# Operand sums of the value products built three half items sooner, with the fourth sum ahead of the first, and two dilated heads begun three half items later

## The chip, the cores and the metric

One core of a Trainium2 chip runs the whole kernel. The time is in device microseconds (us) of that core, from runs of the same program; a profiled execution gives the span and the trace. Engines are named as in the profile: PE (TensorE, matmuls), PEld (its weight loads), DVE (VectorE), ACT (ScalarE), POOL (GpSimd), SP (SyncE, which issues loads).

## The reference

One layer of a decoder trunk on 512 tokens and 1024 channels. Cut to what matters here:

```python
proj = x @ w_in                       # one projection; its columns are q/k/v of three mixers and three gates
(da_q, da_k, da_v, sb_q, sb_k, sb_v, dl_q, dl_k, dl_v, gates) = jnp.split(proj, ...)
o_da = diff_attention(da_q, da_k, da_v, lam, ...)          # 4 heads, two softmax maps each
o_sb = stick_breaking_attention(sb_q, sb_k, sb_v)          # 8 heads
o_dl = dilated_attention(dl_q, dl_k, dl_v, ...)            # 3 groups x 4 heads; groups (128,1),(512,4),(2048,16)
g = sigmoid(gates)
m = (g0 * (o_da @ w_branch_da) + g1 * (o_sb @ w_branch_sb) + g2 * (o_dl @ w_branch_dil)) @ w_out
x = layer_norm(alpha * x + m)
x = layer_norm(alpha * x + relu(x @ w_up)**2 @ w_down + sigmoid(x @ w_ple_gate) * (p @ w_ple))
```

A dilated head slot takes its logits in three groups, softmaxes each, and adds the three group outputs with weights that come from their softmax denominators. The output is float32.

## The kernel before

**Products.** Each float32 operand is split into a high part (ACT casts it to fp32r) and a low part (DVE subtracts), and each product of a 128-row block is three matmuls: high by high, high by low, low by high. Weights come through SP into a ring of 7 tiles `raw`; `split_next` writes the two parts `wh` (L214, ACT) and `wl` (L216, DVE) into rings of 6 tiles each, so a cast waits until PE has left the tile six before it.

**The items.** The work of PE is a list of items, mostly one 128-column or 128-token product of the projection each. The loop at the end of `trunk` goes through them; before each item, and once in the middle of a long one, it calls `step()`, which moves every active generator on to its next `yield`. A `yield` in a generator is therefore half an item of waiting. The attention heads (`sb_head`, `dil_head`, `da_block`) and the helpers in `pending` are such generators. The order that stands in the program on each engine is then made by a scheduler and is fixed; at run time each engine takes its instructions in that order and waits at the first that is not ready.

**The value products.** `value_pair` computes two of the three dilated value projections (`dl_v` 1 and 2) with seven products in place of eight, numbered p and taken in the order 2, 1, 7, 6, 4, 5, 3, each for two token halves r of 12 matmuls (L426 to L428). Products 2, 1 and 3 use x as it is; 7, 6, 4 and 5 need sums of blocks of x. `value_forms` makes these: x comes by POOL's queue into eight tiles `xr` (L353); sum 7 (L376, four DVE instructions), sum 6 (L369), sum 1 (L388, it goes into product 5) and sum 4 (L369 again) go into tiles `fr`, and `parts` casts each to `u7h`, `u6h`, `u4h`, `u5h` on ACT (L239) and takes the low parts `u7l` to `u5l` on DVE (L240). The results are added up by DVE (L436, L440, L441, L443, L447); products 2 and 7 are copied out of their PSUM bank by ACT (L433).

**A dilated head.** `dil_head(hd)` goes in these steps, a `yield` between them: the logits of group 0 on PE (L1589; L1592 in the changed file), whose masked maxima DVE takes (L1592; L1595) and whose exponentials ACT takes; the logits of groups 1 and 2 (L1605; L1608) with DVE's maxima (L1613; L1616); two small products with `fold` and `foldT` (L1630, L1632; L1633, L1635) that bring the statistics of the groups together; a chain of small DVE instructions and one exponential (L1636 to L1652; L1639 to L1655), then eight scalings of the logits (L1654, L1658; L1657, L1661); transposes on PE (L1673, L1682, the same lines in both files) with copies out by ACT and DVE (L98, L100); and the products with the values (L1694, L1699). Heads 0 and 1 run beside the value products.

**Tiles.** Most of these tiles come from one pool of 46 slots of 128x512 (`slot`). A new tile takes a slot that an older one has left, and its first writer waits for the older tile's last reader. PSUM has 2 banks `mm` and 6 banks `at`, with the same rule.

The lines that are not in the functions below:

```python
        RING, RAW = 6, 7
        NSLOT = 46
            if n == v_from[0]:
                pending.append(value_forms())      # four items ahead of value_pair's first
```

## Time and profile before

| | |
|---|---|
| three runs, median | 1066.5 us (1065.89 to 1066.74) |
| profiled execution, its own time | 1067.35 us |
| its span, first to last instruction | 1065.6 us |
| PE, PEld busy | 1049.0 us (98%), 905.1 us (85%) |
| DVE, ACT, POOL busy | 774.1 us (73%), 568.5 us (53%), 145.8 us (14%) |
| granted TensorE clock over the span | 0.995 |

The profiled execution took 0.85 us more than the median; 1.75 us of its time lie outside the span. Busy time is an average over stages. The change touches a stretch from about 225 to 300 us after the span's start, and there the trace has to be read instruction by instruction.

### The profile page before, as it was taken

What the parts mean: (1) busy time and instruction counts of PE and PEld (TensorE: products, weight loads), DVE (VectorE), ACT (ScalarE), POOL (GpSimd) and SP (SyncE); (2) the same over time, 40 slices, a digit from 0 to 9 for tenths busy, and PEclk for the clock granted to TensorE, in tenths of its full rate; (3) what the DMA queues carried; (4) which work ended last, traced back from release to release, by engine and by line L of the source; (5) the groups of instructions that cost most, each with busy time, mean ns of one, the idle gap of its engine ahead of it and who ended that gap; (6) DMA issues with size and microseconds to landing.
All of it is one profiled execution on the core that took longest, in us unless ns stands there. A gap on an engine that the chain in (4) does not pass through costs nothing.

```text
span 1065.6 us, 15588 instructions
## 1 busy us (share of the span) xinstructions
PE 1049.0 (98%) x5802; PEld 905.1 (85%) x5802; DVE 774.1 (73%) x1383; ACT 568.5 (53%) x991; POOL 145.8 (14%) x224
## 2 busy tenths in 40 slices
PE   9999999999899999999999999999999999999996
PEld 6887788889788888888999988888999889889885
DVE  6887667649844757769768773888677877877965
ACT  6665445526432546547535452675756665666641
POOL 0001401220212103230111130100101100100000
PEclk9999999999899999999999999999999999999999
DMA  8346767974898819982676693148888978776602
GB/s 315 111 150 228 168 198 190 306 265 126 234 325 248 241 40 286 243 240 81 204 192 197 180 308 125 62 138 296 225 300 261 242 246 264 244 237 235 196 22 79
DMA packets 63260, 219.75 MB, mean 206 GB/s; under 512 B 7912, under 2 KB 8824, under 8 KB 63184
## 3 DMA queue, kind: packets, MB, share of 16 engines
q1 hardware_dynamic: 37056, 126.80, 34.1%
q0 software_dynamic: 25552, 91.04, 32.9%
q8 instruction: 45, 0.74, 0.3%
q10 hardware_dynamic: 576, 0.92, 0.2%
q14 instruction: 31, 0.25, 0.1%
HBM read 216.61 MB, written 81.81 MB: 280 GB/s over the span
## 4 chain that ended last, share of the span: by engine, by line
PE 88%; DVE 7%; issue 2%; ACT 2%; DMA 0%; POOL 0%; SPq 0%; DVEq 0%; POOLq 0%; ACTq 0%
PE mm L89 13%; PE mm L91 13%; PE mm L90 13%; PE at L89 4%; PE at L1076 4%; PE at L1077 4%; PE at L1078 4%; PE at L91 4%; PE at L90 4%; DVE wl L216 2%; PE mm L458 2%; PE mm L460 2%; PE mm L459 2%; PE at L133 1%; PE at L1467 1%
## 5 line engine op out<-in xcount | busy, mean ns | idle before, releaser
L214 ACT CAST wh<-raw 128x1024 fp32r<-128x1024 f32 x249 | 256.7, 1035 | 262.8 <-PE mm L90 158.7
L216 DVE TENSOR_TENSOR wl<-raw,wh 128x1024 fp32r<-128x1024 f32 x249 | 298.5, 1205 | 99.1 <-ACT wh L214 96.4
L89 PE MATMUL mm<-xhT,wh 128*128 128x512 f32 x368 | 146.7, 399 | 0.0
L91 PE MATMUL mm<-xhT,wl 128*128 128x512 f32 x368 | 144.4, 393 | 0.0
L90 PE MATMUL mm<-xlT,wh 128*128 128x512 f32 x368 | 144.0, 391 | 0.0
L91 PEld LDWEIGHTS mm<-xhT,wl 128*128 128x128 f32 x368 | 69.1, 188 | 15.0 <-DVE wl L216 0.3
L89 PEld LDWEIGHTS mm<-xhT,wh 128*128 128x128 f32 x368 | 69.2, 188 | 13.7 <-issue 0.4
L90 PEld LDWEIGHTS mm<-xlT,wh 128*128 128x128 f32 x368 | 69.2, 188 | 12.9
L1076 PE MATMUL at<-wh,hh 128*128 128x512 f32 x188 | 73.7, 392 | 0.0
L1077 PE MATMUL at<-wl,hh 128*128 128x512 f32 x188 | 73.7, 392 | 0.0
L89 PE MATMUL mm<-x1hT,wh 128*128 128x256 f32 x256 | 73.7, 288 | 0.0
L1078 PE MATMUL at<-wh,hl 128*128 128x512 f32 x188 | 73.1, 389 | 0.0
L90 PE MATMUL mm<-x1lT,wh 128*128 128x256 f32 x256 | 72.3, 283 | 0.0
L91 PE MATMUL mm<-x1hT,wl 128*128 128x256 f32 x256 | 71.9, 283 | 0.0
L89 PEld LDWEIGHTS mm<-x1hT,wh 128*128 128x128 f32 x256 | 48.8, 191 | 4.7 <-ACT up L1010 2.7
L90 PEld LDWEIGHTS mm<-x1lT,wh 128*128 128x128 f32 x256 | 48.9, 191 | 1.5
L914 POOL DMA_DIRECT2D usum<-in_wu_dram x32 | 28.5, 891 | 152.3 <-DVE wl L216 126.6
L91 PEld LDWEIGHTS mm<-x1hT,wl 128*128 128x128 f32 x256 | 48.6, 191 | 0.0
L914 POOL DMA_DIRECT2D dsum<-in_wd_dram x28 | 24.9, 890 | 130.9 <-DVE wl L216 96.2
L1078 PEld LDWEIGHTS at<-wh,hl 128*128 128x128 f32 x188 | 35.3, 188 | 7.7
L1076 PEld LDWEIGHTS at<-wh,hh 128*128 128x128 f32 x188 | 35.5, 189 | 6.0
L1077 PEld LDWEIGHTS at<-wl,hh 128*128 128x128 f32 x188 | 35.5, 189 | 5.5
(516 smaller groups left out, 2666.7 us busy)
## 6 DMA issues: line engine op xcount, KB each, us to landing
usum<-in_wu_dram POOLq DMA_DIRECT2D x48, 512.0 KB, 7.9
raw<-in_wt_dram SPq DMA_DIRECT2D x46, 512.0 KB, 5.1
dsum<-in_wd_dram POOLq DMA_DIRECT2D x42, 512.0 KB, 8.3
raw<-usum SPq DMA_DIRECT2D x32, 512.0 KB, 4.7
raw<-dsum SPq DMA_DIRECT2D x28, 512.0 KB, 4.5
raw<-in_wd_dram SPq DMA_DIRECT2D x25, 512.0 KB, 4.3
raw<-in_wu_dram SPq DMA_DIRECT2D x24, 512.0 KB, 5.2
raw<-in_wv_dram SPq DMA_DIRECT2D x18, 512.0 KB, 8.5
```

The lines of the kernel that those rows point to most:

```text
L89: nc.tensor.matmul(ps, wh, xh, start=start, stop=False, skip_group_check=True)
L90: nc.tensor.matmul(ps, wh, xl, start=False, stop=False, skip_group_check=True)
L91: nc.tensor.matmul(ps, wl, xh, start=False, stop=stop, skip_group_check=True)
L214: i = nc.scalar.copy(h, raw)
L216: i = nc.vector.tensor_sub(lo, raw, h.bitcast(F32))
L458: nc.tensor.matmul(ps, x1, c["h"][:, s], start=k == 0, stop=False)
L459: nc.tensor.matmul(ps, x1, c["l"][:, s], start=False, stop=False)
L460: nc.tensor.matmul(ps, x2, c["h"][:, s], start=False, stop=k == 7)
L914: i = nc.gpsimd.dma_start(o, i, accum_op=OP.add, max_dma_last_dim=4096)
L1076: nc.tensor.matmul(ps, h[:, q], c["h"][:, s], start=go, stop=False, skip_group_check=True)
L1077: nc.tensor.matmul(ps, h[:, q], c["l"][:, s], start=False, stop=False, skip_group_check=True)
L1078: nc.tensor.matmul(ps, lo[:, q], c["h"][:, s], start=False, stop=end, skip_group_check=True)
```

## The change

Sum 7's start comes after 5 waits in place of 8; sum 4 is made before sum 1; dilated heads 0 and 1 wait three more `yield`s before their first logits, and no longer wait two `yield`s between their scalings and their transposes. No instruction is added or removed.

```diff
             parts(6, f6)
             yield
+            f4, o4 = new()
+            for k in range(4):
+                neg_sub(o4[k], o6[k], blk(1, k, 0))
+            yield
+            parts(4, f4)
+            yield
             f1, o1 = new()
             for k in range(4):
                 nc.vector.tensor_sub(o1[k], blk(0, k, 0), blk(0, k, 1))
             yield
-            f4, o4 = new()
-            for k in range(4):
-                neg_sub(o4[k], o6[k], blk(1, k, 0))
-            yield
-            parts(4, f4)
-            yield
             parts(5, f1)
             yield
 
-        WAIT = 8
+        WAIT = 5
...
         def dil_head(hd):
             while any(("dl_q", 4 * g + hd) not in T or ("dl_k", 4 * g + hd) not in T for g in range(3)):
                 yield
+
+            for _ in range(3 if hd < 2 else 0):
+                yield
...
                 nc.vector.tensor_scalar(o, o, mxx[:, c:c + 1], None, op0=OP.mult)
             yield
-            if hd < 2:
-                yield
-                yield
```

In the rows below a name is that of a tile with its number; `L_490`, `L_492` are logits tiles, `st` and `ma` statistics. DVE before, where head 0 begins: its first maxima stand ahead of sum 7 (`fr_2401`).

```order
L293 COPY dl_k_2377<-mm_2346 128x512
L1592 ISA L_490_2381,st_2380<-at_2385,shf_1719 128x128
L1592 ISA st_2380 128x1
L216 TENSOR_TENSOR wl_2372<-raw_1975,wh_2371 128x1024
L1592 ISA L_490_2381,st_2380<-at_2385,shf_1719 128x256
L1592 ISA st_2380 128x1
L1592 ISA L_491_2382,st_2380<-at_2386,shf_1719 128x256
L1592 ISA st_2380 128x1
L1592 ISA L_491_2382,st_2380<-at_2386,shf_1719 128x256
L1592 ISA st_2380 128x1
L376 TENSOR_TENSOR fr_2401<-xr_2186,xr_2182 128x256
```

DVE now, where head 0 begins: sum 4 (`fr_2408`, `fr_2409`, two of its four rows shown) with its low parts, a weight's low part and sum 1 (`fr_2466`, `fr_2467`) stand ahead of the first maxima, and sums 7 and 6 stand some rows further up.

```order
L369 SCALAR_TENSOR_TENSOR fr_2409<-fr_2361,xr_2188 128x256
L369 SCALAR_TENSOR_TENSOR fr_2409<-fr_2361,xr_2189 128x256
L436 TENSOR_TENSOR dl_v_2427<-dl_v_2427,mm_2472 128x512
L240 TENSOR_TENSOR u4l_2431<-fr_2408,u4h_2430 128x512
L216 TENSOR_TENSOR wl_2538<-raw_2239,wh_2537 128x1024
L240 TENSOR_TENSOR u4l_2435<-fr_2409,u4h_2434 128x512
L394 TENSOR_TENSOR fr_2466<-xr_2182 128x256
L394 TENSOR_TENSOR fr_2466<-xr_2183 128x256
L394 TENSOR_TENSOR fr_2467<-xr_2184 128x256
L394 TENSOR_TENSOR fr_2467<-xr_2185 128x256
L1595 ISA L_522_2490,st_2489<-at_2494,shf_1719 128x128
```

Sums 7, 6, 4 and 1 all moved ahead of the heads on DVE; the heads' work moved behind them. Sum 4's first instruction waits for PE in the new program: its two tiles take the slots of one `dl_q` and one `dl_k` tile of head 0, which PE reads in the logits of groups 1 and 2 (L1608). The first maxima of head 1 wait for PE in the same way: their tile takes the slot of a `dl_q` tile that head 1's own logits of groups 1 and 2 read.

PE before, from head 1's `foldT` product on: eight matmuls of products 6 (`mm_2762`) and 4 (`mm_2819`) and four transposes of head 0 are shown, eleven more matmuls of product 4 follow them, and only then head 1's transposes begin.

```order
L1632 MATMUL at_2594<-r_537_2567,foldT 128x32
L428 MATMUL mm_2762<-wh_2499,u6l_2570 128x512
L426 MATMUL mm_2762<-wh_2505,u6h_2573 128x512
L427 MATMUL mm_2762<-wl_2506,u6h_2573 128x512
L428 MATMUL mm_2762<-wh_2505,u6l_2574 128x512
L426 MATMUL mm_2762<-wh_2505,u6h_2573 128x512
L1682 MATMUL at_2734<-ident,L_492_2383 128x128 x2
L1682 MATMUL at_2734<-ident,L_493_2384 128x128 x2
L427 MATMUL mm_2762<-wl_2506,u6h_2573 128x512
L428 MATMUL mm_2762<-wh_2505,u6l_2574 128x512
L426 MATMUL mm_2819<-wh_2640,u4h_2691 128x512
```

PE now, from the last matmul of product 7 on: head 0's transposes (`L_522`), head 1's two fold products, head 0's other transposes and head 1's transposes (`L_547`) follow each other with no product between them.

```order
L428 MATMUL at_2667<-wh_2399,u7l_2336 128x512
L428 MATMUL mm_2819<-wh_2537,u4l_2435 128x512
L1673 MATMUL at_2695<-ident,L_522_2490 128x128 x3
L1673 MATMUL at_2695<-ident,L_523_2491 128x128
L1673 MATMUL at_2702<-ident,L_523_2491 128x128 x3
L1633 MATMUL at_2708<-r_564_2663,fold 128x32
L1635 MATMUL at_2708<-r_565_2665,foldT 128x32
L1682 MATMUL at_2750<-ident,L_524_2492 128x128 x2
L1682 MATMUL at_2750<-ident,L_525_2493 128x128 x2
L1682 MATMUL at_2757<-ident,L_524_2492 128x128 x2
L1682 MATMUL at_2757<-ident,L_525_2493 128x128 x2
L1673 MATMUL at_2764<-ident,L_547_2576 128x128 x3
```

What moved is the work between a head's fold products and its transposes: before it was 19 matmuls of products and four transposes for head 1, now it is eight transposes; for head 0 it is the last ten matmuls of product 7 and one of product 4. SP issues the same loads in the same order; on POOL two loads of table tiles (L1301) stand two places sooner.

## The prediction

> **What bounds the kernel now.** I read the page's first part, then the waits of PE, then the instructions of PE at the two largest of them, then busy time and clock around them, then the other engines there.

> ```profile
> span 1065.6 us, 15588 instructions
> PE 1049.0 (98%) x5802; PEld 905.1 (85%) x5802; DVE 774.1 (73%) x1383; ACT 568.5 (53%) x991; POOL 145.8 (14%) x224
> ```

> PE is the bound, so the time changes only by what PE waits, or runs slower. Of its waits two are over 1.5 us, and both stand in the value products:

> ```profile
> PE mm L426 <- ACT u4h L239: 2.1, 1, 2.1
> PE mm L428 <- DVE u4l L240: 1.5, 1, 1.5
> ```

> Their instructions in order of time (start, duration, in brackets the idle time before and its releaser):

> ```profile
> 266.08 0.40 PE L428 MATMUL mm<-wh,u6l 128*128 128x512 f32 x1
> 268.53 0.50 PE L426 MATMUL mm<-wh,u4h 128*128 128x512 f32 x1 [2.06 <-ACT u4h L239]
> 268.87 0.40 PE L427 MATMUL mm<-wl,u4h 128*128 128x512 f32 x1
> 270.78 0.79 PE L428 MATMUL mm<-wh,u4l 128*128 128x512 f32 x1 [1.52 <-DVE u4l L240]
> 271.38 0.63 PE L426 MATMUL mm<-wh,u4h 128*128 128x512 f32 x1
> ```

> Product 4 comes before its operand is there: PE idles 2.06 + 1.52 = 3.58 us. Busy time in five equal steps around it (PE, PEld, DVE, ACT, POOL, then the granted clock) shows what follows:

> ```profile
> 262.34:265.76 3.42, 3.42 (x22) 2.72 (x20) 3.42 (x8) 1.56 (x2) 0.80 (x1) 1.00 0.37 104
> 265.76:269.17 3.41, 1.35 (x7) 0.57 (x5) 3.41 (x13) 2.97 (x7) 0.00 (x0) 1.00 1.01 251
> 269.17:272.59 3.42, 1.90 (x5) 1.49 (x5) 3.42 (x8) 0.81 (x2) 1.65 (x2) 0.50 0.74 242
> 272.59:276.00 3.41, 3.41 (x11) 2.66 (x10) 2.65 (x10) 0.00 (x0) 0.00 (x0) 0.50 1.07 217
> 276.00:279.40 3.40, 3.40 (x23) 2.98 (x22) 2.35 (x4) 1.68 (x3) 0.00 (x0) 1.00 1.03 263
> ```

> After a step with 1.35 of 3.41 us busy the clock is at half for 6.83 us. Of these PE works 276.00 - 270.78 = 5.2 us and loses half of it, 2.6 us. So at most 3.58 + 2.6 = 6.2 us, 0.6%, can be won here. Why the operand is late shows in DVE, third number of each row:

> ```profile
> 235.00:240.00 5.00, 5.00 (x24) 4.50 (x23) 2.75 (x9) 1.04 (x1) 0.57 (x1) 1.00 0.95 270
> 245.00:250.00 5.00, 5.00 (x32) 4.96 (x32) 5.00 (x31) 3.65 (x12) 0.00 (x0) 1.00 0.00 0
> 260.00:265.00 5.00, 5.00 (x26) 3.96 (x25) 5.00 (x9) 3.90 (x10) 0.80 (x1) 1.00 0.54 152
> ```

> DVE is full there, with sums, weights' low parts and two heads in one queue, and half idle before.

> **The change part by part.** The instructions are the same; their order is what costs. I lay the new order on the durations of this trace: an engine goes on when it is free and what it waits for is done. PE's order is the same in both programs until 237.06. The pieces on PE:

> ```profile
> 237.06 1.68 PE L1589 MATMUL at<-dl_k,dl_q 128*128 128x128 f32 x8
> 238.38 0.60 PE L426 MATMUL mm<-wh,xhT 128*128 128x512 f32 x1
> 241.42 1.95 PE L1605 MATMUL at<-dl_k,dl_q 128*128 128x128 f32 x16
> 243.20 1.68 PE L1589 MATMUL at<-dl_k,dl_q 128*128 128x128 f32 x8
> 256.00 0.40 PE L426 MATMUL mm<-wh,u7h 128*128 128x512 f32 x1
> 258.77 0.93 PE L1673 MATMUL at<-ident,L 128*128 128x128 f32 x7
> 259.45 0.47 PE L426 MATMUL at<-wh,u7h 128*128 128x512 f32 x1
> ```

> A product's twelve matmuls take 258.77 - 256.00 = 2.8 us (0.23 each), a head's second logits 243.20 - 241.42 = 1.8, its first ones 1.3, seven transposes 0.7 (0.1 each). The pieces on DVE:

> ```profile
> 246.70 0.29 DVE L1592 CUSTOM_DVE_ANT_0 L<-at,shf 128x128 f32<-128x128 f32 x1
> 248.01 0.63 DVE L369 SCALAR_TENSOR_TENSOR fr<-fr,xr 128x256 f32<-128x256 f32 x1
> 250.35 1.22 DVE L216 TENSOR_TENSOR wl<-raw,wh 128x1024 fp32r<-128x1024 f32 x1
> 251.49 0.22 DVE L1636 TENSOR_TENSOR sel<-at,pick 128x64 f32<-128x64 f32 x1
> 252.40 0.16 DVE L1646 TENSOR_TENSOR ex<-ot,mxx 128x8 f32<-128x8 f32 x1
> 253.04 0.69 DVE L436 TENSOR_TENSOR dl_v<-dl_v,mm 128x512 f32<-128x512 f32 x1 [0.49 <-PE mm L428]
> 253.65 1.22 DVE L216 TENSOR_TENSOR wl<-raw,wh 128x1024 fp32r<-128x1024 f32 x1
> 256.12 1.07 DVE L1654 TENSOR_SCALAR L<-L,mxx 128x128 f32<-128x128 f32 x4
> 257.11 1.14 DVE L1658 TENSOR_SCALAR L<-L,mxx 128x256 f32<-128x256 f32 x4
> 258.16 0.28 DVE L1613 CUSTOM_DVE_ANT_0 L<-at,shf 128x128 f32<-128x128 f32 x1
> 259.12 0.69 DVE L240 TENSOR_TENSOR u6l<-fr,u6h 128x512 fp32r<-128x512 f32 x1
> 260.40 2.23 DVE L388 TENSOR_TENSOR fr<-xr 128x256 f32<-128x256 f32 x4
> 262.52 1.25 DVE L216 TENSOR_TENSOR wl<-raw,wh 128x1024 fp32r<-128x1024 f32 x1
> ```

> The exponential of a head's chain on ACT, and a `foldT` product on PE:

> ```profile
> 252.59 0.22 ACT L1647 ACTIVATE ex<-ex 128x16 f32<-128x16 f32 x1
> ```

> ```profile
> 250.15 0.30 PE L1632 MATMUL at<-r,foldT 128*128 128x32 f32 x2
> ```

> On DVE, from start to next start: a sum's four instructions 2.1 (260.40 to 262.52), a weight's low part 1.1, a 128x512 add or low part 0.6, four maxima 1.3 (246.70 to 248.01) or, at L1613, 1.0 (258.16 to 259.12), the eight scalings 2.0 (256.12 to 258.16).

> What goes away: sums 7, 6 and 4 stand ahead of the heads now, and sum 1 behind sum 4, so product 4's operand is early and both waits, 3.58 us, fall. Sums 7 and 6 with their low parts, some 6.6 us of DVE, fill idle time before 240 and cost nothing. Late next is what moved behind them, the heads.

> The heads' part. Head 0's first logits come after two products (5.6 us), at 242.7; two more products and its first logits put its second logits at 249.9, the first four of them done at 250.8. Only then is the slot free in which sum 4 is made. DVE stands at that sum until 250.8, with all of head 0 queued behind it. From there it needs 2.1 (sum 4) + 0.6 (L436) + 0.6 + 1.1 + 0.6 (low parts) + 2.1 (sum 1) + 0.55 (two maxima) = 7.65, to 258.5. PE in the meantime:

> - (a) Product 7 wants a bank that product 2's copy on ACT empties late, behind casts that wait for their ring tiles: 0 to 0.7 us, I take 0.5.
> - (b) Head 1's later first logits want head 0's bank, free at 258.5. PE has 0.9 + 0.5 + 2.8 (product 7) + 0.65 + 0.9 (four matmuls of product 6) from 250.8 on, until 256.5: it idles 2.0.
> - (c) Then 0.9 + eight matmuls of product 6, to 261.2; product 4 waits for a bank that L436's sister L440 empties: 0.6 and the hand-over, I take 0.9, to 262.1.
> - (d) Eleven matmuls of product 4 and four of head 1's second logits end at 265.8; they free the slot of head 1's first maxima, at which DVE has stood. From that point to head 0's first scaling took 256.12 - 246.70 = 9.4 us before; four sums (2.2), L436 (0.6) and a wait (0.5) are no longer in it, four maxima more (1.0) are: 7.1, so 273.1 from 266.0 on. PE has the other four logits, twelve matmuls of product 7 and one of product 4, 3.9 us in all, until 269.8. It idles 3.6 for head 0's transposes, with the hand-over.
> - (e) Head 1's `foldT` product wants a statistic that stands behind the eight scalings, 275.2: after seven transposes PE idles 0.8.
> - (f) Head 1's chain then needs 0.6 + 0.5 (an add and a copy ahead of it), 0.9 (251.49 to 252.40), 0.3 for the exponential, about 1.0 for five dependent small instructions at 0.2, and one copy of 0.6: 3.9. PE has eight transposes, 0.9: it idles 3.0.

> The sum is 0.5 + 2.0 + 0.9 + 3.6 + 0.8 + 3.0 = 10.8 us of waits in place of 3.6: +7.2. Bounds for the least certain, (d) and (f): the first cannot vanish while DVE starts at 266 and the scalings need at least four and eight maxima and two low parts (1.3 + 2.0 + 2.2 = 5.5), so 1.9 at the least; (f) is 1.3 at the least by its chain alone without add and copies. Upwards they reach 5.9, with the full 9.4 of before, and 4.5 with two low parts in the chain as head 0 had. The value taken is nearest to what the new queues hold.

> The clock. Between 269.8 and 279.4 PE works some 2 us in 9.6, less than in the step that lost the clock before. The clock goes to half in it, and after the last wait it took 5.2 us before to come back: 2.6 us again. The transposes between are partly hidden behind DVE. (b), 2.0 us of idle, is as long as the 2.06 that counted before, and may bring a spell of its own, 1.7 us for one step of 3.41, one time in two by where the step lies. I take 2.6 + 0.8 = 3.4 against 2.6 now: +0.8. [...]

> POOL's two table loads stand two places sooner and SP's order is kept: POOL is 14% busy, what it loads there is for much later, and I cost them at nothing; uncovered they would be 0.5 us each. After 300 us both orders are the same and PE is full, so the delay stays: +7.2 + 0.8 = +8.0 us.

> **The rivals.**

> A, faster: the changed order only removes the 3.58 us of waiting and its 2.6 us of half clock. It needs a head's chain from fold product to scaling to fit in the PE work beside it, 3 us for head 0 and 1 us for head 1. Head 0's took 6.0 us before, 250.15 to 256.12, so this asks for DVE to be empty then; it decides if the 266.0 start of head 1's maxima comes 4 us earlier. 1066.5 - 6.2 = 1060.3.

> B, even: (a) to (c) vanish since DVE gets ahead in 242 to 250, (d) and (f) shrink to 1.9 and 1.3 with (e): 4.0 against 3.6, and as much half clock. 1066.9.

> C, the waits come as laid, and the clock falls at (b) and stays down from (d) to two steps after (f): 1.7 + 3.4 + 1 of slower transposes against 2.6. 1066.5 + 7.2 + 3.5 = 1077.2.

> [...]

> **How the numbers follow.** The profiled execution took 1067.35, 0.85 above the median; the +8.0 us apply to either, a span of 1073.6 and a median of 1074.5. Chances: as laid 0.58, A 0.08, B 0.09, C 0.15, D 0.10. The forecast's own range is 1070 to 1079.5. The asked range, 1067 to 1080, takes in D and C, half of B, and leaves out A and the far ends, less than 2 in 10. About 0.2%, 2.1 us, is what a measurement of this kernel can tell from no change: slower 0.84, within 0.08, faster 0.08.

> **What would show it.** In the profile after, the two waits of product 4 are gone. PE waits for DVE's scalings at L1673 twice, for some 3 us each, and at the logits of head 1 for some 2 us; DVE is idle for some us between 240 and 251 where it was full; the clock is at 0.5 somewhere between 270 and 286. The prediction is wrong if DVE gets to head 0's scalings before 270, or if sum 4 does not wait for head 0.

## The result, and the profile after

The changed kernel takes 1075.65 us (median of six runs, 1074.23 to 1076.83), the kernel before beside it 1066.5 us (six runs, 1065.89 to 1067.61): a ratio of 1.0084, 95% interval 1.0071 to 1.0097, so 9.15 us slower. The profiled execution took 1074.89 us, 7.54 us more than the profiled one of before. Its page begins:

```profile
span 1073.2 us, 15597 instructions
PE 1049.8 (98%) x5802; PEld 905.7 (84%) x5802; DVE 775.4 (72%) x1383; ACT 570.0 (53%) x991; POOL 146.1 (14%) x224
```

PE has the same 5802 instructions and 0.8 us more busy time; the span is 7.6 us longer. So most of the loss is idle time, and the first view after the page is what PE waited for (us in total, times, longest):

```profile
PE at L1673 <- DVE L L1657: 6.3, 3, 3.6
PE at L1592 <- DVE st L1595: 2.0, 1, 2.0
...
PE mm L426 <- DVE dl_v L440: 0.8, 1, 0.8
...
PE at L1635 <- DVE r L1629: 0.6, 1, 0.6
PE mm L426 <- ACT dl_v L433: 0.4, 1, 0.4
```

The two waits of product 4 for its operand (L239, L240) are gone. In their place PE waits mostly for the heads, twice for a bank of the value products (L440, L433), and for DVE in all but one case. The same waits in order of time, on PE's timeline of the changed kernel:

```profile
252.31 0.50 PE L426 MATMUL mm<-wh,u7h 128*128 128x512 f32 x1 [0.44 <-ACT dl_v L433]
...
258.85 1.13 PE L1592 MATMUL at<-dl_k,dl_q 128*128 128x256 f32 x4 [1.96 <-DVE st L1595]
...
262.61 0.50 PE L426 MATMUL mm<-wh,u4h 128*128 128x512 f32 x1 [0.78 <-DVE dl_v L440]
...
270.30 0.39 PE L428 MATMUL mm<-wh,u4l 128*128 128x512 f32 x1
274.31 1.13 PE L1673 MATMUL at<-ident,L 128*128 128x128 f32 x7 [3.62 <-DVE L L1657]
275.28 0.31 PE L1633 MATMUL at<-r,fold 128*128 128x32 f32 x2
276.16 0.64 PE L1635 MATMUL at<-r,foldT 128*128 128x32 f32 x2 [0.57 <-DVE r L1629]
276.61 1.95 PE L1682 MATMUL at<-ident,L 128*128 128x128 f32 x8
281.07 1.30 PE L1673 MATMUL at<-ident,L 128*128 128x128 f32 x5 [2.51 <-DVE L L1657]
```

They add up to 0.44 + 1.96 + 0.78 + 3.62 + 0.57 + 2.51 = 9.88 us, against 3.58 before. Why the heads are late is seen on DVE's timeline of the same kernel:

```profile
242.44 1.23 DVE L216 TENSOR_TENSOR wl<-raw,wh 128x1024 fp32r<-128x1024 f32 x1 [3.17 <-ACT wh L214]
...
249.33 1.23 DVE L216 TENSOR_TENSOR wl<-raw,wh 128x1024 fp32r<-128x1024 f32 x1 [3.05 <-ACT wh L214]
...
251.01 2.21 DVE L369 SCALAR_TENSOR_TENSOR fr<-fr,xr 128x256 f32<-128x256 f32 x4 [0.46 <-PE at L1608]
...
258.18 0.27 DVE L1595 CUSTOM_DVE_ANT_0 L<-at,shf 128x128 f32<-128x128 f32 x1
...
266.56 0.29 DVE L1595 CUSTOM_DVE_ANT_0 L<-at,shf 128x128 f32<-128x128 f32 x1 [1.87 <-PE at L1608]
...
273.88 1.07 DVE L1657 TENSOR_SCALAR L<-L,mxx 128x128 f32<-128x128 f32 x4
...
278.59 0.69 DVE L100 COPY pt<-at 128x512 f32<-128x512 f32 x1 [0.74 <-PE at L1682]
...
280.63 1.07 DVE L1657 TENSOR_SCALAR L<-L,mxx 128x128 f32<-128x128 f32 x4
```

DVE idles twice for three microseconds ahead of 250; then sum 4 (251.01) starts only when PE has read head 0's second logits (L1608), and head 0's maxima come at 258.18 behind it, head 1's at 266.56. The two long idles are not at sum 4: they are at weights' low parts (L216), whose casts on ACT wait 3.35 and 4.42 us for PE. At sum 4 itself DVE idles 0.46 us, and ACT's copy of product 2 (L433) then waits for sum 4 in its turn, as ACT's timeline shows:

```profile
248.24 1.05 ACT L214 CAST wh<-raw 128x1024 fp32r<-128x1024 f32 x1 [4.42 <-PE mm L428]
...
251.67 0.59 ACT L433 COPY dl_v<-mm 128x512 f32<-128x512 f32 x1 [0.50 <-DVE fr L369]
```

From 245 to 250, where DVE was full before, it works 1.95 of the 5 us now (fourth number of the row, behind the length, PE and PEld):

```profile
245.00:250.00 5.00, 5.00 (x22) 4.86 (x22) 1.95 (x4) 1.05 (x1) 0.62 (x1) 1.00 0.84 199
```

Last, the clock (seventh number), in steps of 3.41 us:

```profile
272.11:275.52 3.41, 1.21 (x9) 1.01 (x9) 3.41 (x10) 3.20 (x11) 1.72 (x2) 1.00 0.44 148
275.52:278.93 3.41, 2.46 (x11) 2.00 (x10) 2.60 (x10) 0.76 (x2) 0.00 (x0) 0.50 0.99 229
278.93:282.35 3.42, 1.28 (x6) 1.30 (x7) 3.00 (x15) 0.37 (x2) 0.00 (x0) 0.50 0.96 224
282.35:285.76 3.41, 3.41 (x11) 2.65 (x10) 0.97 (x3) 0.80 (x2) 0.00 (x0) 0.50 0.07 13
285.76:289.17 3.41, 3.41 (x21) 2.89 (x20) 2.70 (x3) 2.21 (x3) 1.18 (x2) 1.00 0.13 17
```

Three steps run at half clock, 10.24 us, in which PE works 2.46 + 1.28 + 3.41 = 7.15 us. Taken as half of it, the loss is 3.58 us, an estimate: product 6's matmuls start 0.43 us apart at half clock (283.87 to 285.15) and 0.23 at full (285.90 to 286.60). Waits and clock make 9.88 + 3.58 = 13.5 us after and 3.58 + 2.66 = 6.2 us before: 7.2 of the 7.6 us by which the spans differ.

### The profile page after: what moved, and what is told of

Same layout as the page of the kernel before. It is cut to its first block, busy times and chain, and to the rows that moved or that the text cites. A ratio compares the mean times of both kernels' runs of the same rounds, so it can differ in the third digit from the quotient of the medians.

```text
span 1073.2 us, 15597 instructions
## 1 busy us (share of the span) xinstructions
PE 1049.8 (98%) x5802; PEld 905.7 (84%) x5802; DVE 775.4 (72%) x1383; ACT 570.0 (53%) x991; POOL 146.1 (14%) x224
## 4 chain that ended last, share of the span: by engine, by line
PE 87%; DVE 7%; issue 2%; ACT 2%; DMA 0%; POOL 0%; SPq 0%; DVEq 0%; POOLq 0%; ACTq 0%
PE mm L89 13%; PE mm L91 13%; PE mm L90 13%; PE at L89 4%; PE at L1076 4%; PE at L1077 4%; PE at L1078 4%; PE at L91 4%; PE at L90 4%; DVE wl L216 2%; PE mm L458 2%; PE mm L460 2%; PE mm L459 2%; PE at L133 1%; PE at L1467 1%
## 5 line engine op out<-in xcount | busy, mean ns | idle before, releaser
L216 DVE TENSOR_TENSOR wl<-raw,wh 128x1024 fp32r<-128x1024 f32 x249 | 298.5, 1205 | 107.2 <-ACT wh L214 104.5
```

Of the source, the lines that this page charges most:

```text
L216: i = nc.vector.tensor_sub(lo, raw, h.bitcast(F32))
```

## The experiments

Theory H: the loss is the heads' late start, and the largest link in it is the slot by which sum 4 waits for head 0. The rivals put it on the sums' early place, on the two `yield`s taken out ahead of the transposes, or elsewhere than in the slots. Every kernel was timed beside the kernel before in five rounds: 1066.98 us (21 runs) for the first four, 1067.0 us (22 runs) for the others.

**Sums only.** The sums as in the change, the heads as before (both hunks in `dil_head` taken back).

```diff
-            for _ in range(3 if hd < 2 else 0):
-                yield
...
+            if hd < 2:
+                yield
+                yield
```

> The sums as in the change (sum 7 after 5 waits, sum 4 ahead of sum 1), the heads as before. Theory H (the heads' late start is the loss: their DVE work comes too late for PE's next steps, and sum 4's slot hangs on them): most of the change's loss is gone. The new order laid on the measured durations gives one wait of about 4.5 us at head 1's fold product and 1.5 and 0.4 after it, 6.4 in place of 3.6, with one spell of half clock: 1068 to 1070 us. Rival S (the early sums are the loss, since they push the heads back on DVE): as slow as the change, 1074 to 1077.

Measured 1066.77 us, ratio 0.9998 (0.999 to 1.0007). The early sums alone cost nothing, so the rival that blames them falls. It came out some 1.2 us below the range that H expected, mainly since the small waits that H kept did not appear. Nor do the sums win anything: PE's timeline of this kernel has a single wait in the stretch, for a statistic of one head that DVE makes at 259.11, behind the eight scalings of the other (256.80 to 258.84).

```profile
259.35 0.64 PE L1630 MATMUL at<-r,fold 128*128 128x32 f32 x2 [3.76 <-DVE r L1623]
```

**Heads only.** The heads as in the change, the sums as before.

```diff
-        WAIT = 5
+        WAIT = 8
...
+            f1, o1 = new()
+            for k in range(4):
+                nc.vector.tensor_sub(o1[k], blk(0, k, 0), blk(0, k, 1))
+            yield
             f4, o4 = new()
...
-            f1, o1 = new()
-            for k in range(4):
-                nc.vector.tensor_sub(o1[k], blk(0, k, 0), blk(0, k, 1))
-            yield
```

> The heads as in the change (three half items later, no two waits behind the scalings), the sums as before. Theory H: most of the loss is here. Laid on the measured durations: waits of 1.4, 2.8, 1.1, 0.4 and 4.5 us, 10.2 in all; product 4's wait stays among them; one or two spells of half clock: 1072 to 1075. Rival S: near before, 1064 to 1068.

Measured 1075.07 us, ratio 1.007 (1.0056 to 1.0083), just above the range that H expected. The late heads, without the early sums, lose 8.1 us, nearly as much as the whole change. PE's timeline shows product 4's wait for its cast as before, and longer (2.71 us against 2.06), beside the heads':

```profile
259.95 0.41 PE L1633 MATMUL at<-r,fold 128*128 128x32 f32 x2 [1.42 <-DVE r L1626]
...
267.97 0.79 PE L426 MATMUL mm<-wh,u4h 128*128 128x512 f32 x1 [2.71 <-ACT u4h L239]
...
280.47 1.42 PE L1673 MATMUL at<-ident,L 128*128 128x128 f32 x7 [4.38 <-DVE L L1657]
```

**Two `yield`s kept.** The change, with the two `yield`s between scalings and transposes put back.

```diff
             yield
+            if hd < 2:
+                yield
+                yield
```

> The change with the two half items between scalings and transposes kept for heads 0 and 1, so that all of both heads is three half items later. Theory H: it is as slow as the change; the two waits at the transposes (3.6 and 2.5) only join in one place, some 6.5 to 7 us, with the earlier ones (0.4, 2.0, 0.8) unchanged: 1074 to 1077. Rival Y (the loss comes from taking the two half items away, which put the transposes right behind the scalings): 1065 or less, product 4's wait and both waits at the transposes gone.

Measured 1076.04 us, ratio 1.0078 (1.0065 to 1.009). Taking them out is not the loss. PE's timeline shows that the waits at the scalings have come together in one place instead; the four ahead of it have the changed kernel's sizes within 0.04 us.

```profile
283.30 1.73 PE L1676 MATMUL at<-ident,L 128*128 128x128 f32 x7 [6.56 <-DVE L L1657]
```

**Sum 4 in tiles that are free.** The change, with sum 4 written over sum 7's tiles, which are read by then, in place of new ones from the pool. Its link to head 0 is gone. The two slots that it no longer takes go to other tiles, and the scheduler makes another order from this, so the run does not test the link alone.

```diff
-            f4, o4 = new()
+            f4, o4 = f7, o7
```

> The change, with sum 4 written into sum 7's tiles, which are read out by then, in place of two new tiles. So sum 4 no longer takes the slots of head 0's dl_q and dl_k. Theory H with the slot as its first link: DVE does not stand 0.5 to 3 us at sum 4, head 0's maxima come some 4 us earlier, the waits at product 7, at head 1's logits and at product 4 shrink to 0.6, the two at the transposes to 2.4 and 3.2: 6.2 of waits in place of 9.9, 1069 to 1072. Rival L (the slot is beside the point, DVE is just full later): no change against the change itself, 1074 to 1077.

Measured 1069.69 us, ratio 1.0022 (1.0013 to 1.0031), as H expected: 6 of the 9 us come back for one line, and the rival to which the slot was beside the point falls. On DVE's timeline sum 4 starts right behind sum 6 now and ends before four low parts of weights (L216) that stood ahead of it, and head 1's maxima come 6.2 us sooner than in the changed kernel:

```profile
233.80 3.26 DVE L369 SCALAR_TENSOR_TENSOR fr<-fr,xr 128x256 f32<-128x256 f32 x6
...
239.29 0.64 DVE L369 SCALAR_TENSOR_TENSOR fr<-fr,xr 128x256 f32<-128x256 f32 x1
239.82 1.24 DVE L216 TENSOR_TENSOR wl<-raw,wh 128x1024 fp32r<-128x1024 f32 x1
...
260.39 0.29 DVE L1595 CUSTOM_DVE_ANT_0 L<-at,shf 128x128 f32<-128x128 f32 x1 [0.52 <-PE at L1608]
```

Head 0's maxima start at 253.12, 5.1 us sooner. Of that the wait at sum 4 can have given 0.46 at most, since in the changed order the weight's low part ahead of it held DVE until 250.56; the rest came with the new order. Two waits for scalings are left on PE, and two steps at half clock with them:

```profile
268.93 1.29 PE L1673 MATMUL at<-ident,L 128*128 128x128 f32 x5 [1.98 <-DVE L L1657]
...
275.87 1.29 PE L1673 MATMUL at<-ident,L 128*128 128x128 f32 x5 [3.07 <-DVE L L1657]
```

**Sums 4 and 1 in tiles that are free.** The same for sum 1, which takes sum 6's tiles.

```diff
-            f4, o4 = new()
+            f4, o4 = f7, o7
...
-            f1, o1 = new()
+            f1, o1 = f6, o6
```

> The change with sum 4 in sum 7's tiles and sum 1 in sum 6's, so that no sum takes a slot of a head's tiles. Theory H with slots: what the slots cost is gone on DVE, the heads' late start is left: one wait of some 4 us at head 1's transposes and one spell of half clock: 1065.5 to 1068.5, between the run with sum 4 alone (1069.7) and before (1067.0). Rival L2 (the tiles of sum 1 do not matter): as with sum 4 alone, 1069 to 1070.5.

Measured 1066.37 us, ratio 0.9996 (0.9987 to 1.0004). With both sums in free tiles the late heads cost nothing any more; the rival that expected only sum 4's tiles to matter falls. The order on DVE is another one again: sum 1 stands at 241.44, ahead of head 0's maxima at 248.19. What sum 1's place gave, and what its slots, this run does not part; in the run with sum 4 alone in free tiles DVE does not wait at sum 1. One wait is left on PE's timeline, near the size that product 4's two had together before (3.58 us):

```profile
272.94 1.73 PE L1673 MATMUL at<-ident,L 128*128 128x128 f32 x7 [4.00 <-DVE L L1657]
```

**No late start.** The change without the three `yield`s ahead of the heads; the two later ones stay out.

```diff
-            for _ in range(3 if hd < 2 else 0):
-                yield
```

> The change without the three half items ahead of heads 0 and 1; the two half items behind the scalings stay away, the sums stay as changed. Theory H (the late start of the heads is the loss): laid on the measured durations, waits of 2.3 and 1.1 us at head 0's transposes and head 1's fold product and 3.0 at a product, 6.4 in all against 9.9 of the change, with one or two spells of half clock: 1067.5 to 1070.5. Rival Y (taking the two half items away is the loss): 1074 or more.

Measured 1068.91 us, ratio 1.0018 (1.0008 to 1.0027). Of the 9 us, 7 come back with the three `yield`s, which agrees with heads only; the rival that blames the two later `yield`s, and expected 1074 or more, falls. In the profiled execution PE waits 1.64, 1.07 and 2.72 us, where H had 2.3, 1.1 and 3.0.

**Sum 4 first, and nothing else.** The kernel before with sum 4 ahead of sum 1.

```diff
             parts(6, f6)
             yield
+            f4, o4 = new()
+            for k in range(4):
+                neg_sub(o4[k], o6[k], blk(1, k, 0))
+            yield
+            parts(4, f4)
+            yield
             f1, o1 = new()
...
-            f4, o4 = new()
-            for k in range(4):
-                neg_sub(o4[k], o6[k], blk(1, k, 0))
-            yield
-            parts(4, f4)
-            yield
```

> Only sum 4 ahead of sum 1; sums begin after 8 waits and heads as before. Theory H: it takes sum 1's 2.1 us out of product 4's way: waits of 1.8 at product 4 and 1.2 at head 1's transposes, 3.0 in place of 3.6, with half the spell of half clock or none: 1063.5 to 1066. Rival N (sum 4's place is worth nothing, product 4 waits for its cast and not for its sum): 1066.5 to 1067.5.

Measured 1063.57 us, ratio 0.9972 (0.9961 to 0.9983), at the lower end of what H expected; the rival to which sum 4's place is worth nothing falls. PE waits 1.45 us at product 4, for a bank (L433) and no longer for the operand, and 0.77 at head 1's transposes, and no step is at half clock.

**Sum 4 first, sums four half items sooner.** As the last, with an earlier start.

```diff
-        WAIT = 8
+        WAIT = 4
```

> Sum 4 ahead of sum 1, sums after 4 waits in place of 8, heads as before: the version that the new order, laid on the measured durations, gives the least waits. Theory H: 0.7 us at head 0's foldT product and 1.3 at head 1's transposes, 2.0 in place of 3.6, and no spell of half clock, whose 2.7 us are won too: 1061 to 1064. Rival S2 (sums ahead of the heads push these back as in the run with sums after 5 waits, which gained nothing): 1066 to 1068.

Measured 1062.61 us, ratio 0.9961 (0.9948 to 0.9973), within what H expected: the fastest version of this study. Of PE's waits in the stretch one is left on its timeline, and no step at half clock:

```profile
270.18 1.23 PE L1673 MATMUL at<-ident,L 128*128 128x128 f32 x7 [0.91 <-DVE L L1654]
```

So with the heads as before and sum 4 first, an earlier start of the sums does not act in proportion: 8 waits give 1063.57 us, 5 give 1066.77 (sums only) and 4 give 1062.61. Where the scheduler sets a sum among the heads' work decides, as in the wait of 3.76 us of sums only.

The ten kernels can be set beside each other by what PE idles between 225 and 300 us and what it loses at half clock there (half of the time that it works in such steps, an estimate as above), all from profiled executions:

| kernel | idle, us | lost to the clock, us | sum against before | span against before |
|---|---|---|---|---|
| before | 3.6 | 2.7 | | |
| changed | 9.9 | 3.6 | +7.2 | +7.6 |
| sums only | 3.8 | 1.6 | -0.9 | -1.2 |
| heads only | 8.5 | 4.9 | +7.1 | +6.7 |
| two `yield`s kept | 10.4 | 2.4 | +6.5 | +7.1 |
| sum 4 in free tiles | 5.5 | 3.4 | +2.7 | +2.0 |
| sums 4 and 1 in free tiles | 4.0 | 1.5 | -0.7 | -1.3 |
| no late start | 5.4 | 0 | -0.8 | 0.0 |
| sum 4 first | 2.2 | 0 | -4.0 | -4.0 |
| sum 4 first, four sooner | 1.0 | 0 | -5.3 | -5.1 |

The sum follows the span within 0.8 us everywhere, so the rest of the kernel is not in it. The row of no late start stands for a short execution, 1067.32 us where the median is 1068.91: it has no step at half clock, and what its longer runs lost is not in the table.

## Why the prediction was right

The forecast was 1074.5 us, the median is 1075.65, and for the profiled execution 1067.35 + 8.0 = 1075.35 against 1074.89. The mechanism held at the places it named: sum 4 waits for head 0 (251.0 against 250.8), head 0's maxima come at 258.2 (258.5), head 1's at 266.6 (266.0), the scalings at 273.9 (273.1). At the first of these places luck helped. The forecast had DVE stand at sum 4 until 250.8; DVE stood most of that time at weights' low parts, for casts that ACT made late, until 250.56, and then 0.46 us at sum 4. So in this order the slot sets the start by less than half a microsecond; what a free slot in the same order would have been worth was not tried. The terms by name, in us:

| term | forecast | measured |
|---|---|---|
| (a) product 7's bank | 0.5 | 0.44 |
| (b) head 1's logits | 2.0 | 1.96 |
| (c) product 4's bank | 0.9 | 0.78 |
| (d) head 0's transposes | 3.6 | 3.62 |
| (e) `foldT` | 0.8 | 0.57 |
| (f) head 1's transposes | 3.0 | 2.51 |
| clock | 3.4 | 3.58 |
| all, less 6.2 of before | +8.0 | +7.2 |

The single sizes that were off belong together. In (f) the eight transposes were put at 0.9 us; they ran at half clock and took from 276.61 to 278.56, 1.95 us. That hides more of head 1's chain, and it also delays the copy at 278.59, for which DVE idles 0.74 us and which stands in the middle of the chain: so (f) fell by half a microsecond, not by a whole one. Term (a) has its size, but the last thing that the copy of product 2 waited for was sum 4 (0.50 us, L369), not a cast. The clock's sum was near by luck, for its working was not right: no spell followed (b), for which 0.8 was put in, and the spell at (d) was three steps long, with 7.15 us worked in it and not 5.2. The forecast had told of that half clock from (d) to behind (f), and had then priced only what came after the last wait. The POOL loads cost nothing that the traces show.

The rivals. A, faster, fell, and its point of decision was wrong too: with sum 4 in free tiles head 1's maxima start 6.2 us sooner, more than the 4 us that A asked for, and the kernel is still slower, 1.0022 times the time before, since both heads' scalings keep PE waiting for 1.98 and 3.07 us. B, even, asked for (a) to (c) to vanish and 4.0 us to stay at the transposes. The version with both sums in free tiles comes near it: it has 4.00 us of waiting there, though in one place and not in three, and takes 1066.37 us where B's working gave 1066.9. So B describes another kernel, and what parts it from this one are the tiles of two sums and the order that follows from them. Of C, the part behind (d) is near what the trace shows: the clock stays down until 285.76, 4.7 us or 1.4 steps behind the end of (f), where C had two. Its spell at (b) is not in the profiled execution, where the step from 255.04 to 258.45 holds 1.85 us of PE work; had one step held all of the 1.96 us of idle, it would have had 1.45, between the 1.43 that lost the clock elsewhere and the 1.57 that kept it. Whether the slowest runs of the changed kernel (1076.83 us at a mean clock of 0.989, against 1074.23 at 0.994) had a spell there was not seen. D, at 0.10 in the forecast, fell: it had the clock back within (f), where the trace has it at half throughout (275.52 to 285.76).

The prediction named one more thing than the runs bear out. It set the late heads and the slot link side by side as parts of one path; heads only, at 1075.07 us, loses nearly as much without the early sums, and in its trace DVE works 3.31 of the 3.41 us from 264.03 on, ahead of product 4's late operand, which leaves 0.10 us there for a wait for a slot. So late heads lose in two different ways: behind early sums whose tiles hang on them, and ahead of late sums, where product 4 waits for its operand as well. With both sums early and in free tiles they lose nothing. What the slots decide when the sums are left late was not tried.

## What to carry to other kernels

When work is moved sooner in a queue, look at what its output tile takes over: here a sum's tiles came from operands of the very head that the same change delayed, and one line that gave it tiles already free was worth 6 us. The wait itself was less than half a microsecond; look as well at the order that the scheduler makes out of such a link, which moved the sum ahead of four other instructions here. Read what is moved behind as closely as what is moved ahead: making the operand that PE waited for sooner was worth 3.4 to 4.4 us by itself, and delaying the heads cost 8. Count idle time of PE by steps of the clock, not by gaps.

## What the runs showed of the hardware

```profile
264.83:268.24 3.41, 2.52 (x11) 1.71 (x10) 3.41 (x7) 2.84 (x6) 0.80 (x1) 1.00 0.12 23
268.24:271.65 3.41, 1.59 (x10) 1.36 (x11) 3.34 (x14) 0.00 (x0) 0.00 (x0) 1.00 1.03 268
271.65:275.07 3.42, 3.42 (x23) 2.94 (x22) 2.50 (x6) 2.39 (x4) 0.00 (x0) 1.00 0.47 165
```

PE is busy 2.52 and 1.59 us (second number) and the clock stays full. The kernel with sum 4 in free tiles has a gap of 1.98 us in one step:

```profile
265.65:269.06 3.41, 1.43 (x7) 0.89 (x5) 3.38 (x11) 3.18 (x10) 1.66 (x2) 1.00 0.29 74
269.06:272.47 3.41, 3.41 (x18) 3.37 (x18) 2.25 (x8) 0.59 (x1) 0.00 (x0) 0.50 1.02 256
272.47:275.89 3.42, 0.35 (x4) 0.14 (x2) 2.57 (x13) 0.80 (x2) 0.00 (x0) 1.00 1.04 259
```

There 1.43 us busy is followed by half clock, and behind one step with 3.41 us of PE work the clock is full again. Cut into steps from their own spells, the kernel before and the changed one over their whole length, and sums only, heads only, two `yield`s kept and both kernels with free tiles around their long waits, show 11 full-clock steps with 0 to 1.43 us of PE work. Each is followed by half, and none of those with 1.57 or more is. The 1.57 is in the kernel before, near its end:

```profile
1054.23:1057.65 3.42, 1.57 (x14) 1.37 (x12) 3.35 (x10) 0.00 (x0) 0.19 (x1) 1.00 0.41 153
```

For the way back, heads only has a step that does not reach:

```profile
264.03:267.44 3.41, 1.23 (x6) 0.69 (x4) 3.31 (x23) 3.23 (x10) 0.00 (x0) 1.00 0.01 2
267.44:270.85 3.41, 2.88 (x11) 2.27 (x12) 3.41 (x18) 2.42 (x4) 0.00 (x0) 0.50 0.00 0
270.85:274.26 3.41, 3.41 (x14) 3.12 (x15) 3.41 (x7) 3.07 (x11) 1.08 (x2) 0.50 0.14 22
```

Sums 4 and 1 in free tiles has one that does:

```profile
272.51:275.92 3.41, 2.98 (x11) 2.70 (x12) 2.68 (x9) 0.59 (x1) 0.00 (x0) 0.50 0.51 107
275.92:279.33 3.41, 3.41 (x21) 2.89 (x20) 1.52 (x2) 2.26 (x3) 0.00 (x1) 1.00 0.00 0
```

After 2.88 us busy at half clock the next step is at half too; after 2.98 it is full again. The other half-clock steps of these kernels in the stretch agree: those with 1.28 to 2.46 us are followed by half, those with 3.16 and 3.41 by full. Nothing was measured between 2.88 and 2.98, and busy times of PE are modelled.

The length of the gap alone does not order these runs: the gap of 1.98 us lost the clock and the one of 2.72 us did not.

The steps lay elsewhere in each of these executions: in the rows above they begin at 264.83, 265.65 and 264.03 us. If the place of the steps decides, a kernel with a gap that can fall into one step or across two should spread, and one without should not; this was the author's estimate. The gap of 2.72 us of no late start, all in one step, would leave 0.69 us of work in it, an estimate from the rows. The runs fit: with no late start they reach from 1066.71 us, at a mean clock of 0.998, to 1070.74, at 0.992, over ten runs, and the fastest version, which has no step at half clock in the stretch, from 1062.17 to 1062.92 over five. That the longer runs lost clock is thus on record; that the place of the steps is the cause was argued, not tested.
